# A four-layer decoder trunk: the two head-pair phases of its delta-rule layer become one timetable of 16 jobs

## The chip, the cores and the metric

The kernel runs on one core of one Trainium2 chip. The metric is the device time of one execution in microseconds, the median of the runs. Each core has a TensorE for matmuls (PE in the profile, its weight loads PEld), a VectorE (DVE), a ScalarE (ACT), a GpSimd (POOL) and a SyncE (SP) that issues the transfers.

## The reference

Four layers run one after the other over 1024 tokens of 1024 channels: a gated short convolution, a diagonal state-space layer, a delta-rule layer, and a second convolution. After each mixer come a gated embedding and a LayerNorm. Only the third layer's mixer is touched. Cut to what matters:

```python
def _rwkv_step(state, inp):
    r_t, w_t, k_t, v_t, kk_t, a_t = inp
    sa = jnp.einsum("bhvk,bhk->bhv", state, -kk_t)
    state = (state * w_t[:, :, None, :] + sa[..., None] * (kk_t * a_t)[:, :, None, :]
             + v_t[..., None] * k_t[:, :, None, :])
    return state, jnp.einsum("bhvk,bhk->bhv", state, r_t)

def rwkv7_mixer(x, ...):                    # 16 heads of 64
    xs = x[None] + dx[None] * mu[:, None, None, :]          # six mixes of x with its shift
    r, k, v, z = jnp.einsum("nbld,nde->nble", xs[:4], w_rkvz)
    w_log = -softplus(-(w0 + tanh(xs[4] @ w1) @ w2)) - 0.5   # the decay, low rank
    a = sigmoid(a0 + (xs[5] @ a1) @ a2)
    kk = normalised(k * k_k);  k = k * (1 + (a - 1) * k_a)
    _, out = lax.scan(_rwkv_step, s0, (r, decay, k, v, kk, a))   # over 1024 tokens
    out = group_norm(out) * lnx_g + lnx_b + sum(r * k * r_k) * v
    return (out * silu(z)) @ w_out
```

## The kernel before

All data is float32. A projection of 512 tokens onto 128 channels is 24 matmuls of 128x512: the weights and the inputs are each split into a rounded high part and a rest, and three of the four products are summed over eight blocks of 128 input channels. `wsplit_hi` (a ScalarE cast of 128x1024) and `wsplit_lo` (a VectorE subtraction) split a block of weights, and `build` mixes, splits and stores eight blocks of an input (`xs3`, `xs2`, `xs1`, `xs0` for z, v, k, r).

The recurrence is computed in chunks of 64 tokens. The 1024 tokens fall into two halves of 512, the 16 heads into eight pairs that fill 128 partitions, so there are 16 jobs of one pair and one half, of eight chunks each. A job goes through four stages in four successive slots:

- as `c` it gets its key projection (`K`, psum `kps`) and the decays, and begins its receptance projection (`Rd`);
- as `b` it gets scaled keys `kb`, queries `ra`, the chunk scores `s1`, their masks and the bonus;
- as `a` the triangular matrices of its chunks are inverted: `solve` and `unfold` on VectorE, then `join1` to `join4` and `queries`, each some tiny matmuls whose result ScalarE copies to SBUF for the next;
- as `s` it runs the chunks one after the other: `read` is a matmul with the state, whose result ScalarE copies (`uv`), and `update` a second matmul, from which two VectorE instructions (L2173) make the new state.

In the slot behind that its outputs are normalised (`g`). A slot has 16 steps: an even one begins with `read`, an odd one with `update`. Within a slot the table of steps in `phase` sets the order on every engine, and `pin` holds the scheduler to it; outside `phase` a scheduler places what is ready. `phase(h, ...)` runs eight jobs of one half in 11 slots, n = -3 to 7, since four jobs are under way at once. It is called twice. In its last three slots, where no new projections start, it is given others to do (`fill`): in the first call the z projections of half 1, in the second the output projections of half 0.

The layer's order is: `lora(0)` (the two low-rank products), z and v of half 0, with `decay` for each channel block; `phase(0)`; `lora(1)`, v and decay of half 1; `phase(1)`; then output projection, gate and LayerNorm. z, v, decays and the bonus go through DRAM. PSUM has eight banks: two for projections (`pmm`), three for small products (`paux`), and in `pseq` two for a job's outputs (`p1`) and one for `update`.

Of the kernel before, what the change touches and what calls it, by code (L numbers as in the profile page):

```python
# [1349 lines left out]
def rwkv_layer(S, X, bg, l, last, nxt):  # L1350
# [136 lines left out]
    def k_decays(m, h, R):  # L1487
# [7 lines left out]
        SC.activation(R.kp, R.ga, AF.Identity, scale=vec("k_a")[:, m:m + 1], bias=C.oka[:, m:m + 1])
        G.tensor_tensor(R.ga, R.ga, R.cs, ALU.mult)

    def k_evac(m, h, R):
# [3 lines left out]
        V.scalar_tensor_tensor(c3(R.aq), c3(ps), C.nkk[:, m:m + 1], R.pt[:, :, 0:CH], ALU.mult, ALU.mult)
        SC.activation(R.kk, ps, AF.Copy, scale=vec("k_k")[:, m:m + 1])
# [51 lines left out]

    def r_low(R):
        G.tensor_tensor(R.kl, R.kp, f32(R.kh), ALU.subtract)
# [707 lines left out]
```

## Time and profile before

| | us |
|---|---|
| median of 3 runs (lowest, highest) | 2899.98 (2897.66, 2902.37) |
| the profiled execution | 2900.2 |
| its span, first to last instruction | 2898.5 |
| DVE / ACT / POOL busy in the span | 1796.8 / 1122.3 / 670.0 |
| delta-rule mixer, first projection to first gate matmul | 1145.6 to 2147.7 |
| phase 0, first to last `read` | 1352.7 to 1656.1 |
| phase 1, first to last `read` | 1833.9 to 2124.7 |

The layer is read in stretches, from one `read` of a slot's step 0 to the next: a view that gives the busy time of each engine in each stretch shows where it is slow. TensorE's busy time counts overlapping matmuls and their modelled ends, so it says little by itself. The granted clock of TensorE (PEclk, 1.00 is full) stands in the same rows.

### The profile page before, as it was taken

What the parts mean: (1) busy time and instruction counts of PE and PEld (TensorE: products, weight loads), DVE (VectorE), ACT (ScalarE), POOL (GpSimd) and SP (SyncE); (2) the same over time, 40 slices, a digit from 0 to 9 for tenths busy, and PEclk for the clock granted to TensorE, in tenths of its full rate; (3) what the DMA queues carried; (4) which work ended last, traced back from release to release, by engine and by line L of the source; (5) the groups of instructions that cost most, each with busy time, mean ns of one, the idle gap of its engine ahead of it and who ended that gap; (6) DMA issues with size and microseconds to landing.
All of it is one profiled execution on the core that took longest, in us unless ns stands there. A gap on an engine that the chain in (4) does not pass through costs nothing. (4 is left out here: it accounts for less than half of the span.)

```text
span 2898.5 us, 47059 instructions
## 1 busy us (share of the span) xinstructions
PE 2698.8 (93%) x18331; PEld 2162.0 (75%) x18331; DVE 1796.8 (62%) x3288; ACT 1122.3 (39%) x2154; POOL 670.0 (23%) x828
## 2 busy tenths in 40 slices
PE   8999999999999999978887986988889999999998
PEld 6887887778878887666775764777667778888887
DVE  6777865477657348866676486666657573333654
ACT  3333322242154124655555474555534231111322
POOL 1243413222107043004344101344232210000000
PEclk9999999999999999988887998999999999999999
DMA  5333322267873334542222353222234332112311
GB/s 165 100 97 92 97 71 66 88 179 208 224 239 106 102 91 131 164 160 84 73 86 80 119 156 119 76 80 90 94 111 137 109 88 58 51 44 66 117 64 39
DMA packets 449775, 313.09 MB, mean 108 GB/s; under 512 B 48360, under 2 KB 393744, under 8 KB 449552
## 3 DMA queue, kind: packets, MB, share of 16 engines
q1 hardware_dynamic: 449552, 310.08, 35.5%
q8 instruction: 144, 2.36, 0.3%
q14 instruction: 79, 0.65, 0.1%
HBM read 240.28 MB, written 69.21 MB: 107 GB/s over the span
## 5 line engine op out<-in xcount | busy, mean ns | idle before, releaser
L300 DVE TENSOR_TENSOR wl<-wraw,wh 128x1024 fp32r<-128x1024 f32 x283 | 367.1, 1298 | 338.9 <-ACT wh L292 332.8
L292 ACT CAST wh<-wraw 128x1024 fp32r<-128x1024 f32 x283 | 296.4, 1048 | 650.7 <-PE gp L335 189.7
L2173 DVE SCALAR_TENSOR_TENSOR state<-state,pc,p 64x64 f32<-64x64 f32 x256 | 70.9, 277 | 81.0 <-PE p L2170 76.6
L2164 PE MATMUL p<-state,ra 128*128 128x128 f32 x256 | 62.5, 329 | 52.7 <-DVE state L2173 52.7
L672 POOL TENSOR_TENSOR ln_s<-ln_s,rp 128x512 f32<-128x512 f32 x42 | 60.0, 1428 | 210.4 <-DVE rp L668 210.4
L2164 PEld LDWEIGHTS p<-state,ra 128*128 128x128 f32 x256 | 44.4, 205 | 79.5 <-DVE state L2173 72.9
L2165 ACT COPY uv<-p 64x128 f32<-64x128 f32 x128 | 33.1, 258 | 141.5 <-PE p L2164 140.4
L334 PE MATMUL gp<-r_0h,wh 128*128 128x512 f32 x192 | 76.8, 400 | 0.9 <-ACT yt L2226 0.9
L336 PE MATMUL gp<-r_0h,wl 128*128 128x512 f32 x192 | 77.3, 403 | 0.0
L334 PE MATMUL zp<-x_0h,wh 128*128 128x512 f32 x192 | 76.8, 400 | 0.0
L335 PE MATMUL gp<-r_0l,wh 128*128 128x512 f32 x192 | 76.7, 400 | 0.0
L334 PE MATMUL gp<-r_1h,wh 128*128 128x512 f32 x192 | 76.3, 397 | 0.0
L336 PE MATMUL gp<-r_1h,wl 128*128 128x512 f32 x192 | 76.0, 396 | 0.0
L336 PE MATMUL zp<-x_0h,wl 128*128 128x512 f32 x192 | 75.9, 395 | 0.0
L334 PE MATMUL zp<-x_1h,wh 128*128 128x512 f32 x192 | 75.9, 395 | 0.0
L336 PE MATMUL zp<-x_1h,wl 128*128 128x512 f32 x192 | 75.7, 394 | 0.0
L335 PE MATMUL zp<-x_0l,wh 128*128 128x512 f32 x192 | 75.7, 394 | 0.0
L335 PE MATMUL zp<-x_1l,wh 128*128 128x512 f32 x192 | 75.6, 394 | 0.0
L335 PE MATMUL gp<-r_1l,wh 128*128 128x512 f32 x192 | 75.4, 393 | 0.0
L687 POOL TENSOR_TENSOR rp<-r_0h,r_0l 128x512 f32<-128x512 f32 x24 | 37.4, 1590 | 163.3 <-PE op L335 162.9
L2170 PEld LDWEIGHTS p<-uv,kbt 128*128 128x128 f32 x256 | 49.2, 209 | 25.5 <-ACT uv L2165 17.5
L2170 PE MATMUL p<-uv,kbt 128*128 128x128 f32 x256 | 56.4, 305 | 11.5 <-ACT uv L2165 11.5
(760 smaller groups left out, 8392.4 us busy)
## 6 DMA issues: line engine op xcount, KB each, us to landing
wraw<-in_conv_w_in_dram SPq DMA_DIRECT2D x80, 512.0 KB
wraw<-in_rwkv_w_rkvz_dram SPq DMA_DIRECT2D x64, 512.0 KB
wraw<-in_ple_gate_dram SPq DMA_DIRECT2D x56, 512.0 KB
wraw<-in_conv_w_out_dram SPq DMA_DIRECT2D x24, 512.0 KB
wraw<-in_ssm_w_in_dram SPq DMA_DIRECT2D x21, 512.0 KB
xt<-xd SPq DMA_DIRECT2D x32, 256.0 KB
wraw<-in_rwkv_w_out_dram SPq DMA_DIRECT2D x16, 512.0 KB
wraw<-in_ple_proj_dram SPq DMA_DIRECT2D x14, 512.0 KB
```

The lines of the kernel that those rows point to most:

```text
L292: S.nc.scalar.copy(wh, raw)
L300: S.nc.vector.tensor_tensor(wl, raw, f32(wh[:]), ALU.subtract)
L334: nc.tensor.matmul(ps, lh, xh, start=(k == 0), stop=False)
L335: nc.tensor.matmul(ps, lh, xl, start=False, stop=False)
L336: nc.tensor.matmul(ps, ll, xh, start=False, stop=(k == kt - 1))
L672: nc.gpsimd.tensor_tensor(s, s, rs, ALU.add)
L687: (eng or nc.gpsimd).tensor_tensor(rs, f32(rh[:]), f32(rl[:]), ALU.add)
L2164: nc.tensor.matmul(p1, R.ra[:, c, :], R.st, start=False, stop=False, skip_group_check=True)
L2165: SC.copy(R.uv[w][rb, c2, :], p1[rb, :])
L2170: nc.tensor.matmul(p2[:, 0:P], R.kbt[c // 4][:, c % 4, :], R.uv[w][:, c2, :], start=True, stop=True)
L2173: V.scalar_tensor_tensor(R.st[cs, cs], R.st[cs, cs], R.pc[cs, c:c + 1], p2[cs, cs], ALU.mult, ALU.add)
```

## The change

Both halves go through one `phase` of 16 jobs in 19 slots, n = -3 to 15; the job of a half 1 pair takes its state from DRAM as before. z of both halves and v of both halves are computed ahead of it, and v's weights are loaded and split once for both halves. The fill of the last three slots is the output projection of half 0 alone, by a table `NE`; `NK` and `NR` spread the 24 matmuls of K and R over other steps. The inputs of half 1 (`xs1`, `xs0`) are built inside slots 5 and 6, those of r of half 0 in slot -3.

Inside a slot nearly everything moves to another step. A product and the copy of its result out of PSUM become two functions (`join1` and `join1_out`, and so on), and a weight block's cast (`high`, steps 4 and 9) and subtraction (`low`, steps 7 and 13) stand apart. `solve` 3 moves from step 15 to the next slot's step 1, `solve` 0 from step 14 to step 13, the joins from steps 5 to 8 to steps 8 to 13, `queries` from 10 to 14. `p1` shares a pool of five banks with the small products.

Some instructions change: the ScalarE copy `kk` goes, and VectorE multiplies `kps` itself; the second copy of `queries` goes from VectorE to ScalarE; every job takes the group norm's root from ScalarE's Ln and Exp with a refinement on GpSimd, where jobs with m of 5 and more had another routine; the rest `kl` of the bonus is computed twice, by two equal GpSimd instructions.

```diff
-            for h in range(2):
-                for i in (3, 2):
-                    blocks("rwkv_w_rkvz", (0, i))
+            for i in (3, 3, 2):
+                blocks("rwkv_w_rkvz", (0, i))
+            for h in range(2):
...
-    S.paux = pss.enter_context(S.tc.tile_pool(name="paux", bufs=3, space=PSUM))
+    S.paux = pss.enter_context(S.tc.tile_pool(name="paux", bufs=5, space=PSUM))
...
     def k_evac(m, h, R):
-        SC.activation(R.kk, ps, AF.Copy, scale=vec("k_k")[:, m:m + 1])
...
+    def k_keys(m, R):
...
+        kk = T_("kk")
+        V.scalar_tensor_tensor(kk, R.kps, vec("k_k")[:, m:m + 1], R.ga, ALU.mult, ALU.mult)
...
+        V.tensor_tensor(view(R.kb, 0, [[256, 4], [192, 2], [1, 64]]), c4(kk), c4(prn), ALU.mult)
...
     def r_bonus(m, h, R):
...
         G.tensor_tensor(R.kl, R.kp, f32(R.kh), ALU.subtract)
 
+        G.tensor_tensor(R.kl, R.kp, f32(R.kh), ALU.subtract)
...
-    def phase(h, builds, fill, late):
+    def phase(fill, work):
...
+        def high():
+            if len(S.wready) + len(S.whalf) <= 1 and len(S.worder) > len(S.wready) + len(S.whalf):
+                wsplit_hi(S)
+                wnext(S)
+
+        def low():
+            if S.whalf:
+                wsplit_lo(S)
...
+        NR = 4, 4, 6, 6, 0, 0, 0, 0, 0, 0, 0, 0, 0, 2, 0, 2
+        NK = 0, 0, 0, 0, 3, 6, 6, 1, 2, 1, 0, 3, 2, 0, 0, 0
...
-        for n in range(-3, NB):
+        for n in range(-3, NP):
...
     def queries(R):
...
-        SC.copy(r5[:, :, 0, acol[0]], ps[0][:, 0:256].rearrange("p (c t) -> p c t", c=4))
-        V.tensor_copy(r5[:, :, 1, acol[1]], ps[1][:, 0:256].rearrange("p (c t) -> p c t", c=4))
+    def queries_out(R):
+        r5 = R.ra.rearrange("p (c w) s -> p c w s", w=2)
+        for w in range(2):
+            SC.copy(r5[:, :, w, acol[w]], R.pq[w][:, 0:256].rearrange("p (c t) -> p c t", c=4))
...
     def values(R):
-        R.p1 = [S.pseq.tile([P, 4, P], F32, tag="p1", name="p1", bufs=2) for w in range(2)]
+        R.p1 = [aux("p1").rearrange("p (a b) -> p a b", a=4) for w in range(2)]
...
+    for m in range(NB):
+        use_z(m, 0, zv_mm(zw(m), 3, m, 0))
+        pull(bg, ZP[m])
+    L = [lora(0)]
+    while bg:
+        pull(bg)
+    x1_load()
+    for _ in build(S, X, 3, 1):
+        pass
+    nxt_b.append(build(S, X, 2, 0))
+    for m in range(NB):
+        use_z(m, 1, zv_mm(zw(m), 3, m, 1))
+        decay(m, 0, L[0])
+        pull(nxt_b)
...
+    L.append(lora(1))
+    for _ in build(S, X, 2, 1):
         pass
+    for m in range(NB - 2):
+        w = vw(m)
+        for h in range(2):
+            use_v(m, h, zv_mm(w, 2, m, h))
+        decay(m, 1, L[1])
...
+    spread(build(S, X, 0, 0), -3, (1,) * 8, 4)
+    work[(NB - 4, 14)] = [x1_load]
+    spread(build(S, X, 1, 1), NB - 3, (2, 2, 1, 1, 1, 1), 4)
+    spread(build(S, X, 0, 1), NB - 3, (1, 1, 1, 1, 1, 1, 2), 12)
+    spread(ys_build(0), 2 * NB - 4, (1, 0, 0) + (1,) * 8, 13)
+    phase(wos, work)
```

How the order moves at three places. First VectorE in the middle of a slot, around the state's instruction (L2173 before, L2228 now, two 64x64 halves in a row); `wl` is the weight subtraction, `sca` the masked scores, `ra` the queries, `kp` the bonus product. Before:

```order
L1550 SCALAR_TENSOR_TENSOR kp<-sp,vec_174,kp 128x512
L2173 SCALAR_TENSOR_TENSOR state<-state,pc,p_13550 64x64 x2
L1980 TENSOR_TENSOR sca<-s_13578,mask 128x4x64
L1980 TENSOR_TENSOR sca<-s_13577,mask 128x4x64
L300 TENSOR_TENSOR wl<-wraw,wh 128x1024
L2173 SCALAR_TENSOR_TENSOR state<-state,pc,p_13636 64x64 x2
L1980 TENSOR_TENSOR sca<-s_13641,mask 128x4x64
L1980 TENSOR_TENSOR sca<-s_13640,mask 128x4x64
L2138 COPY ra<-a_13667 128x4x64
L2173 SCALAR_TENSOR_TENSOR state<-state,pc,p_13693 64x64 x2
```

Now:

```order
L2228 SCALAR_TENSOR_TENSOR state<-state,pc,p_14378 64x64 x2
L1554 SCALAR_TENSOR_TENSOR kp<-sp,vec_174,kp 128x512
L2006 TENSOR_TENSOR sca<-s_14386,mask 128x4x64
L2006 TENSOR_TENSOR sca<-s_14385,mask 128x4x64
L300 TENSOR_TENSOR wl<-wraw,wh 128x1024
L2228 SCALAR_TENSOR_TENSOR state<-state,pc,p_14463 64x64 x2
L2006 TENSOR_TENSOR sca<-s_14468,mask 128x4x64
L2006 TENSOR_TENSOR sca<-s_14467,mask 128x4x64
L2228 SCALAR_TENSOR_TENSOR state<-state,pc,p_14567 64x64 x2
L2038 STREAM_TRANSPOSE mi<-dg 128x1024
```

The subtraction `wl` stands ahead of the state of chunk 4 in both; before, it was step 8's, now it is step 7's `low`, whose cast is from step 4 (below). The copy `ra<-a` is gone from this queue.

Second ScalarE, around that weight block's cast `wh` (L292 before, L293 now); `uv` is the copy that follows a `read`, `tt`, `t` and `zi` belong to the joins, `kph` to the bonus, `gsq` or `junk` to the group norm. Before, from step 6 to step 9:

```order
L1552 CAST kph<-kp 128x512
L2197 ACTIVATE gsq,gn_q<-o 128x64
L2117 COPY t_13535<-zp 32x256 x2
L1982 COPY scr<-s_13578 128x4x64
L1982 COPY scr<-s_13577 128x4x64
L1342 ACTIVATE rs_t<-gn_q 128x8
L1343 ACTIVATE gn_s<-rs_t 128x8
L2165 COPY uv<-p_13263 64x128
L2125 COPY tt<-tp 32x8x32 x2
L292 CAST wh<-wraw 128x1024
L1993 COPY dg<-sca 32x256 x2
```

Now, from step 4 to step 8:

```order
L2220 COPY uv<-p_14184 64x128
L2253 ACTIVATE junk,gn_q<-o 128x64
L293 CAST wh<-wraw 128x1024
L2121 COPY uv<-wps 64x512 x2
L2253 ACTIVATE junk,gn_q<-o 128x64
L2220 COPY uv<-p_14185 64x128
L2253 ACTIVATE junk,gn_q<-o 128x64
L1556 CAST kph<-kp 128x512
L2253 ACTIVATE junk,gn_q<-o 128x64
L2220 COPY uv<-p_14184 64x128
```

The cast stood in the step of its subtraction, behind the copies of `join3`, the scores and `join4`; now it stands three steps ahead of it, behind one instruction of the group norm.

Third TensorE, at the joins: `zi`, `ut`, `zp` are the products of `join1` to `join3`, `p` is `read` (from state) or `update` (from uv), `sp` a projection. Before:

```order
L2087 MATMUL zi<-t_12288,nz_9823 32x32 x32
L2089 MATMUL zi<-ident 32x256 x4
L370 MATMUL sp<-xs1h,wh 128x512
L370 MATMUL sp<-xs1l,wh 128x512
L370 MATMUL sp<-xs1h,wl 128x512
L2164 MATMUL p_12164<-state,ra 128x128
L2098 MATMUL ut<-zi,ub 32x32 x32
L2101 MATMUL ut<-ub,zi 32x32 x32
L370 MATMUL sp<-xs1h,wh 128x512
L370 MATMUL sp<-xs1l,wh 128x512
L2170 MATMUL p_12450<-uv,kbt 128x128
L2115 MATMUL zp<-t_12435,m_11949 32x32 x16
```

Now, where `join2` and `join3` stand:

```order
L2219 MATMUL p_13636<-state,ra 128x128
L2142 MATMUL ut<-zi,ub 32x32 x32
L2145 MATMUL ut<-ub,zi 32x32 x32
L2225 MATMUL p_14018<-uv,kbt 128x128
L1565 MATMUL pb<-kph,c_ones_r 128x512
L1566 MATMUL pb<-kpl,c_ones_r 128x512
L371 MATMUL sp<-xs1l,wh 128x512
L371 MATMUL sp<-xs1h,wl 128x512
L371 MATMUL sp<-xs1h,wh 128x512
L2280 MATMUL otp<-ident,o 128x128 x4
L2219 MATMUL p_13635<-state,ra 128x128
L2164 MATMUL zp<-t_14022,m_13286 32x32 x16
```

Between `join2` and `join3` there stood two projection matmuls and an `update`; now there stand three, the bonus sum `pb`, four transposes `otp`, an `update` and a `read`.

More of the change, by code (lines that the diff above doesn't have):

```diff
@@ L25 @@
 VECS = {}
+AHEAD = 2
 class Ctx:
@@ L304, in wnext @@
 def wnext(S, ahead=2):
-    while len(S.wraws) < ahead and len(S.wready) + len(S.wraws) < len(S.worder):
+    while len(S.wraws) < ahead and len(S.wready) + len(S.whalf) + len(S.wraws) < len(S.worder):
         wdma(S)
@@ L1074 @@
 IP, TP, TQ = 5,2,2
-AHEAD = 2
 NU = 5
@@ L1783, in phase @@
                     if b:
+                        I.solve(b, 1)
                         I.solve(b, 2)
-                        I.solve(b, 3)
-                if n in (-3, 5) and i >= 4:
-                    thunk()
+                    if g:
+                        I.gate(g)
                 pin()
-        g = Rs[NB - 1]
+        g = Rs[NP - 1]
         I.square(g, 0, 8)
-        I.norm(g, h)
+        I.norm(g)
+        I.refine(g)
         I.scale(g)
@@ L1794, in phase @@
         I.affine(g)
-        I.gate(g, h)
+        I.gate(g)
         pin()
@@ L1893, in rwkv_layer, with spread @@
                  **w_out_then(m)) for m in range(NB)]
-    phase(1, build(S, X, 0, 1), wos, ys_build(0))
+    work = {}
+    def spread(g, n, counts, first=0):
+        for j, c in enumerate(counts):
+            for _ in range(c):
+                work.setdefault((n + (first + j) // 16, (first + j) % 16), []).append(lambda: next(g, None))
+    spread(build(S, X, 0, 0), -3, (1,) * 8, 4)
[4 more added lines that the diff above has]
+    phase(wos, work)
     while wos:
@@ L2226, in affine, with gate @@
         SC.activation(q4(R.yt), q4(R.po)[:, :, ::-1, :], AF.Identity, scale=gn[:, m:m + 1], bias=bn[:, m:m + 1])
-    def gate(R, h):
+    def gate(R):
         G.tensor_tensor(R.yt, R.yt, R.bv, ALU.add)
         G.tensor_tensor(R.yt, R.yt, R.z, ALU.mult)
-        nc.sync.dma_start(dY[R.m][:, h * HT:(h + 1) * HT], R.yt)
-    I.scores, I.mask, I.low_mask, I.diag, I.fold, I.scale_keys, I.kbt = scores, mask_, low_mask, diag, fold, scale_keys, kbt
-    I.solve, I.unfold, I.corr, I.corr_out = solve, unfold, corr, corr_out
-    I.join1, I.join2, I.join3, I.join4, I.queries, I.values = join1, join2, join3, join4, queries, values
-    I.init, I.read, I.update, I.outputs = init, read, update, outputs
-    I.square, I.norm, I.scale, I.turn, I.affine, I.gate = square, norm, scale, turn, affine, gate
+        nc.sync.dma_start(dY[R.m][:, R.h * HT:(R.h + 1) * HT], R.yt)
+    for f in (scores, low_mask, diag, off_diag, fold, scale_keys, loads, kbt, kbt_out, solve, unit, unfold, corr, corr_out,
+              join1, join1_out, join2, join2_out, clear, join3, join3_out, join4, join4_out, queries, queries_out, init, values,
+              read, update, outputs, outputs_out, square, norm, refine, scale, turn, affine, gate):
+        setattr(I, f.__name__, f)
+    I.mask, I.mask_r = mask_a, mask_r
     return I
```

502 lines of the change are left out of this document (250 added, 252 removed).

## The prediction

> **What bounds it now.** The page's head gives the span; the profiled execution took 2900.2 us, 0.01% from the runs' median of 2899.98, so the sum is made against 2900.2. About 6 us (0.2%) is what a measurement here can tell from no change.
>
> The view of stretches comes first, since only the delta-rule mixer is touched: per stretch its length, the busy time of each engine, the granted clock, and the transfers. The first 21 rows are slots and prologues in the order of the program (the last two of the fence are the first prologue).
>
> ```profile
> span 2898.5 us, 47059 instructions
> ...
> 1270.00:1352.70 82.70, 61.35 (x621) 48.09 (x619) 48.45 (x98) 42.78 (x78) 24.78 (x33) 0.79 0.29 91
> 1352.70:1388.30 35.60, 31.49 (x539) 25.25 (x535) 24.14 (x69) 18.91 (x43) 12.11 (x17) 1.00 0.19 57
> 1388.30:1427.40 39.10, 35.68 (x540) 29.09 (x538) 23.49 (x53) 22.14 (x62) 16.75 (x25) 0.87 0.20 67
> 1427.40:1469.20 41.80, 36.15 (x543) 29.32 (x539) 26.58 (x65) 22.15 (x62) 16.73 (x25) 0.88 0.25 79
> 1469.20:1508.20 39.00, 34.29 (x541) 27.76 (x539) 26.71 (x65) 22.04 (x62) 16.71 (x25) 0.91 0.28 84
> 1508.20:1548.20 40.00, 34.19 (x541) 28.19 (x539) 26.81 (x65) 22.03 (x62) 16.71 (x25) 0.91 0.43 135
> 1548.20:1601.20 53.00, 36.05 (x510) 28.80 (x506) 38.22 (x90) 27.39 (x71) 16.62 (x23) 0.68 0.20 59
> 1601.20:1635.10 33.90, 31.59 (x516) 25.60 (x512) 15.18 (x45) 17.44 (x47) 5.26 (x9) 1.00 0.33 104
> 1635.10:1670.00 34.90, 31.39 (x179) 24.49 (x177) 16.29 (x48) 15.37 (x53) 5.12 (x6) 1.00 0.46 137
> 1670.00:1690.00 20.00, 11.98 (x34) 4.18 (x34) 17.00 (x24) 17.20 (x28) 2.87 (x2) 0.84 0.42 124
> 1690.00:1745.30 55.30, 55.30 (x243) 43.53 (x243) 44.32 (x67) 36.45 (x68) 0.00 (x0) 0.96 0.54 176
> 1745.30:1833.90 88.60, 61.05 (x630) 46.90 (x628) 53.34 (x107) 45.59 (x84) 24.67 (x32) 0.83 0.30 103
> 1833.90:1868.90 35.00, 31.51 (x538) 25.49 (x534) 24.20 (x67) 19.02 (x43) 10.97 (x16) 1.00 0.21 63
> 1868.90:1906.30 37.40, 32.96 (x543) 26.95 (x539) 23.82 (x53) 22.05 (x62) 16.56 (x24) 0.95 0.21 69
> 1906.30:1945.30 39.00, 32.90 (x540) 26.90 (x538) 26.66 (x65) 22.05 (x62) 16.60 (x24) 0.96 0.26 85
> 1945.30:1987.60 42.30, 37.18 (x542) 30.58 (x538) 26.66 (x65) 22.14 (x62) 16.59 (x24) 0.84 0.24 78
> 1987.60:2026.50 38.90, 33.19 (x543) 26.77 (x539) 26.82 (x65) 22.04 (x62) 16.57 (x24) 0.96 0.31 92
> 2026.50:2066.50 40.00, 30.89 (x509) 24.63 (x507) 30.75 (x78) 21.81 (x63) 16.59 (x21) 0.83 0.36 115
> 2066.50:2100.60 34.10, 32.03 (x514) 25.42 (x512) 18.44 (x52) 16.21 (x46) 4.44 (x6) 1.00 0.27 86
> 2100.60:2137.00 36.40, 31.90 (x174) 25.35 (x173) 18.71 (x43) 15.21 (x52) 8.48 (x8) 0.95 0.35 109
> 2137.00:2147.70 10.70, 1.61 (x8) 0.79 (x6) 9.50 (x12) 1.89 (x3) 7.99 (x7) 0.69 0.48 148
> 1145.60:1233.00 87.40, 80.32 (x323) 54.58 (x322) 76.78 (x125) 54.30 (x95) 14.50 (x23) 0.96 0.53 163
> 1233.00:1270.00 37.00, 37.00 (x175) 29.84 (x174) 29.78 (x40) 22.70 (x34) 0.00 (x0) 1.00 0.71 232
> sum 1002.10, PE 841.98 PEld 658.50 DVE 672.65 ACT 548.89 POOL 287.65; mean PE 36.61 PEld 28.63 DVE 29.25 ACT 23.86 POOL 12.51
> ```
>
> The mixer takes 1002.1 us. Its eight full slots (n = 1 to 4 of each phase) take 39.7 us on average, and no engine fills one: DVE 24 to 27, ACT 22, POOL 17; PE's 33 to 37 counts overlaps and slow clock. So a slot is bound by waits in turn, not by an engine. The two ramps, in which the first job climbs three stages, cost 82.7 and 88.6 us.
>
> The same view by chunk (two steps each), for the slot that starts at 1987.6:
>
> ```profile
> 1987.60:1992.60 5.00, 2.73 (x24) 2.20 (x20) 4.78 (x19) 2.67 (x7) 1.27 (x1) 1.00 0.73 204
> 1992.60:1995.70 3.10, 2.57 (x12) 1.87 (x12) 2.88 (x8) 2.03 (x8) 0.00 (x0) 1.00 0.01 3
> 1995.70:2000.80 5.10, 4.58 (x114) 3.55 (x115) 4.90 (x11) 1.36 (x7) 0.00 (x0) 1.00 0.37 104
> 2000.80:2005.30 4.50, 4.41 (x183) 3.77 (x181) 0.62 (x3) 3.83 (x13) 1.85 (x3) 1.00 0.20 66
> 2005.30:2010.80 5.50, 3.56 (x57) 2.90 (x56) 2.79 (x5) 3.54 (x10) 3.79 (x9) 1.00 0.01 3
> 2010.80:2016.40 5.60, 5.58 (x50) 4.45 (x51) 2.54 (x7) 2.86 (x7) 3.68 (x7) 0.70 0.42 117
> 2016.40:2018.80 2.40, 2.40 (x13) 1.76 (x11) 2.32 (x3) 1.93 (x4) 0.19 (x1) 1.00 0.66 192
> 2018.80:2026.50 7.70, 7.37 (x94) 6.26 (x93) 5.99 (x12) 3.81 (x8) 5.78 (x4) 1.00 0.21 78
> ```
>
> A chunk can pass in 2.40 us. Chunks 0 and 2 are VectorE's (4.78 of 5.00, 4.90 of 5.10), 3 is TensorE's joins and scores, and in 4 nobody works through. The timeline shows why, and what slows VectorE in the last chunk of another slot, the one from 1868.9 (the fence ends with two groups of the four slots from there: busy us, mean ns, idle before):
>
> ```profile
> 2008.70 1.56 DVE L300 TENSOR_TENSOR wl<-wraw,wh 128x1024 fp32r<-128x1024 f32 x1 [2.64 <-ACT wh L292]
> ...
> 2010.82 0.49 PE L2164 MATMUL p<-state,ra 128*128 128x128 f32 x2 [1.97 <-DVE state L2173]
> ...
> 1900.13 1.90 POOL L2005 TENSOR_TENSOR kb<-kb,pc 128x1024 f32<-128x1024 f32 x1
> ...
> 1901.62 1.98 DVE L2036 TENSOR_TENSOR tp<-mi 128x192 f32<-128x192 f32 x2
> 1903.53 1.71 DVE L2039 TENSOR_TENSOR mi<-mi,tp 128x192 f32<-128x192 f32 x2
> ...
> L1557 POOL TENSOR_TENSOR kpl<-kp,kph 128x512 fp32r<-128x512 f32 x4 | 5.1, 1266 | 0.6 <-ACT kph L1552 0.3
> L1503 ACT ACTIVATE kk<-sp,vec 128x512 f32<-128x512 f32 x4 | 2.8, 690 | 3.6 <-DVE aq L1502 3.6
> ```
>
> `wl` waits 2.64 us for its cast, the state's instruction stands behind it, and `read` waits 1.97 us for the state. In the chunk after, the clock is 0.70.
>
> **The steady slot, from 39.7 us.** Removed: (a) the cast now stands three steps ahead of `wl`; of 2.64 us I take 2.0. (b) With that gap gone the slow chunk runs at full clock; 5.6 us at 0.70 is 3.9 at 1.00, and I take 1.2 of the 1.7. (c) The joins are spread from steps 5 to 8 over 8 to 14, each copy with a dense product or a read behind it; chunks 2 and 3 (9.6 us) lose 1.5. (d) In the last chunk 10 of its 12 projection matmuls go elsewhere (10 x 0.228 = 2.3 us, the 0.228 being 55.30 us over 243 in the row of v), `solve` 3 moves to step 1, and `solve` 0's four products (1.98 + 1.71) now stand ahead of GpSimd's big multiply; of some 4 us I take 2.5, since ScalarE now has nine copies in steps 13 to 15. Added: (e) chunks 0 and 1 get 20 of R's matmuls where eight stood, 12 x 0.228 = 2.7, of which VectorE's 4.78 and 2.88 there cover all but 1.0; (f) in step 14 `queries` takes two of the three banks that `p1` leaves free, as before, but `otp` now sits in the third until `affine`; `pss` behind it has to wait for a bank, and behind `pss` stand `update`, ScalarE and the state. I take 0.5, between 0 and the 1.97 that is the nearest wait shown. The ScalarE copy `kk` (0.69) goes and one of 128x256 comes; both lie beside a VectorE that is the later of the two. The second `kl` adds 1.27 us to a GpSimd that is busy 16.6 of 39: nothing. Balance: 39.7 - 2.0 - 1.2 - 1.5 - 2.5 + 1.0 + 0.5 = 34.0 us. The bounds: no gain, 39.7, and 31.0, if (a) to (d) give their full 2.6, 1.7, 2.0 and 4.0 and (e) and (f) 1.6.
>
> **The prologues.** z of half 0 had 87.4 us together with the low-rank products, decays and the previous layer's LayerNorm on a VectorE that was busy 76.78. Without the first two, 192 matmuls take 44 us and VectorE some 40: I take 50 (44 to 62). The low-rank stage now stands alone as half 1's did, 20.0 us (VectorE 17.00 of it), and the reading back of x adds 3: 23, bounds 14 and 30. z of half 1 with decays, 224 matmuls: 53, like the 55.3 of v with decays. The second low-rank stage: 20. v of both halves: 55.3 and another 192 x 0.228 = 44, less a first product under the low-rank stage: 95; the eight weight splits saved lie under it and are worth nothing. Sum 241, where 124.4 + 20 + 55.3 = 200 stood: z of half 1 is no longer under a phase's tail.
>
> **The phase.** One ramp, the mean of the two rows, 85 (75 to 95: same chains, other steps). Slot 0 at 35.3 x 34.0 / 39.7 = 30. Twelve full slots, n = 1 to 12: 408. The 16 inputs that slots 5 and 6 build: the 53.0 of slot 5, which built eight, against 39.7 is 13; VectorE's own part 38.22 - 26.7 = 11.5; half of the second eight lies in slot 6 under less: 20, bounds 12 and 27. The last three slots with the output projections, 40.0 + 34.1 + 36.4 = 110.5, less the gain of two slots: 99. The step to the gate stays, 10.7. Their queue of transfers moves too: key loads go from step 5 to step 2, v's from the transposes to step 0, all on SP, with a slot's 70 to 135 GB/s far from the 232 of a row above.
>
> Sum: 241 + 85 + 30 + 408 + 20 + 99 + 10.7 = 893.7, against 1002.1: -108, so 2792. Each us of the slot is worth about 15 (12 slots, and the outer ones in part).
>
> [...]
>
> **Rivals.** First, the slots stay at 39.7: the chain of `read`, copy, `update`, state may find another late partner at each place where one was removed, ScalarE above all. For it: no engine was full, so the waits may only wander. Against: (a) is a named wait whose cause moves away. The time: 15 x 5.7 = 85 more, 2878; still faster, since a ramp of 85 and the tail are saved and 41 given back.
>
> Second, the second `kl` counts: it runs in step 7 with `wl`, which reads two tiles of SBUF and took 1.56 at 2008.70 beside GpSimd's work; held up by 1.27 in each of 16 slots, ahead of the state, it costs 20: 2812.
>
> Third, slower: TensorE waits more often with fewer projections near its joins, and the granted clock falls in all slots as in slot 5, the row with 0.68 and 53.0 us. From a slot of 41.2 on (34.0 + 108 / 15) the gain is gone; TensorE's 33 us busy at 0.96 would be 41 at 0.77, so a mean of 0.77 decides. At 0.72 a slot is 44: 2942. Against: the slots of 33.9 and 34.1 us ran at 1.00, and full ones at 0.95 with the gap of (a) in them. [...]
>
> **Chances.** Forecast, slots of 31.5 to 37: 0.60, 2792, its own range 2755 to 2838. Slots unchanged: 0.16. The lock: 0.10. The slow clock: 0.14, of which 0.03 fall within 0.2%. Faster 0.86, the same 0.03, slower 0.11. The range takes in the unchanged slots above and slots of 31 below: 2745 to 2880, with 0.08 below and 0.12 above left out.
>
> **What would show it.** In the stretches: 12 slots of 33 to 35 us with the clock above 0.95; `wl` without a wait for `wh`; chunk 4 at 3.6 or less, the last at 5 to 6; a prologue of 235 to 250 us up to the first K product; one ramp of 85. The forecast is wrong if slots pass 37, if slot 5 exceeds 65, or if z of half 1 waits long for its inputs behind x's read-back.

## The result and the profile after

The changed kernel takes 2923.85 us against 2899.45 of the kernel before (medians): a ratio of 1.0081, 95% interval 1.0061 to 1.0101. It is slower by 0.8%, where 2792 us, 3.7% faster, had been forecast. The profiled execution took 2923.56 us. One of the four runs was in a slow state (3090.82 us at a mean clock of 0.823, where the other three had 0.951 or 0.952) and is left out of the ratio; the other three took 2922.15 to 2924.13.

The view of stretches, kernel after, in the same form as in the prediction (length; busy us of PE, PEld, DVE, ACT, POOL; granted clock; transfers). First the gap, z of half 0, the low-rank products, z of half 1, the low-rank products again, v, and the ramp:

```profile
1145.60:1152.70 7.10, 0.86 (x4) 0.38 (x2) 7.10 (x9) 4.12 (x6) 6.40 (x13) 0.80 0.69 163
1152.70:1206.60 53.90, 50.14 (x213) 39.67 (x213) 38.21 (x63) 17.78 (x27) 7.72 (x12) 0.96 0.55 174
1206.60:1222.60 16.00, 10.98 (x32) 3.94 (x32) 14.04 (x21) 14.13 (x24) 0.00 (x0) 0.86 0.63 187
1222.60:1284.90 62.30, 56.41 (x224) 42.99 (x224) 46.55 (x71) 42.50 (x78) 0.00 (x0) 0.91 0.53 171
1284.90:1300.00 15.10, 15.08 (x46) 5.12 (x48) 10.76 (x16) 9.16 (x15) 0.00 (x0) 0.84 0.01 5
1300.00:1406.00 106.00, 101.38 (x460) 80.47 (x456) 52.09 (x78) 39.76 (x74) 0.00 (x0) 0.98 0.43 149
1406.00:1495.30 89.30, 57.84 (x612) 44.29 (x612) 61.83 (x108) 50.99 (x94) 28.59 (x35) 0.83 0.28 88
```

Then slots of the one phase: n = 0, 1, 4, 5, 6, 9, 10, 13, and the last with the step to the gate:

```profile
1495.30:1528.60 33.30, 30.57 (x539) 25.58 (x535) 27.27 (x70) 18.58 (x43) 14.50 (x19) 1.00 0.19 59
1528.60:1570.70 42.10, 37.46 (x540) 31.78 (x538) 23.52 (x63) 22.24 (x63) 19.02 (x26) 0.83 0.22 70
1652.00:1694.10 42.10, 37.49 (x541) 31.93 (x539) 23.40 (x62) 22.19 (x62) 18.99 (x26) 0.82 0.40 129
1694.10:1760.70 66.60, 45.47 (x540) 35.82 (x538) 43.73 (x86) 37.07 (x86) 20.19 (x26) 0.71 0.17 54
1760.70:1809.00 48.30, 39.65 (x540) 32.59 (x538) 30.25 (x70) 26.95 (x70) 18.75 (x26) 0.82 0.18 60
1890.80:1933.00 42.20, 37.55 (x541) 31.98 (x539) 23.39 (x62) 22.21 (x62) 18.84 (x25) 0.82 0.25 78
1933.00:1972.60 39.60, 34.90 (x540) 29.77 (x538) 23.79 (x62) 22.09 (x62) 18.75 (x25) 0.89 0.27 85
2056.20:2093.70 37.50, 31.52 (x521) 25.45 (x519) 28.84 (x61) 23.07 (x65) 16.94 (x22) 0.89 0.30 93
2126.90:2171.00 44.10, 32.32 (x182) 25.46 (x180) 20.23 (x31) 18.54 (x58) 18.90 (x24) 0.92 0.43 131
```

VectorE's work in a full slot is 23.4 to 23.8 us (24 to 27 before), and yet the slots are longer: 41.3 us on average for the ten without builds, against 39.7, with a clock of 0.82 to 0.89. In n = 0, where no group norm runs yet, the clock is 1.00. The chunks of the slot from 1890.8 show where:

```profile
1890.80:1896.50 5.70, 5.70 (x31) 5.25 (x30) 1.45 (x4) 1.85 (x4) 1.15 (x1) 0.72 0.55 176
1896.50:1899.70 3.20, 3.20 (x17) 2.67 (x16) 2.54 (x9) 2.14 (x10) 0.13 (x1) 1.00 0.23 82
1899.70:1903.50 3.80, 3.80 (x46) 3.23 (x45) 2.78 (x11) 2.86 (x8) 0.00 (x0) 1.00 0.02 4
1903.50:1906.90 3.40, 3.40 (x29) 2.85 (x28) 3.23 (x9) 0.61 (x3) 0.00 (x0) 1.00 0.00 0
1906.90:1910.60 3.70, 3.70 (x97) 2.80 (x96) 2.66 (x7) 1.94 (x7) 2.82 (x2) 1.00 0.16 49
1910.60:1917.70 7.10, 5.13 (x142) 4.21 (x141) 3.10 (x5) 5.61 (x14) 6.46 (x14) 0.78 0.18 53
1917.70:1920.90 3.20, 3.19 (x74) 2.64 (x73) 1.78 (x4) 2.16 (x5) 0.85 (x3) 0.96 0.22 82
1920.90:1933.00 12.10, 9.44 (x116) 8.34 (x114) 5.86 (x19) 5.03 (x12) 7.42 (x8) 0.66 0.33 100
```

Chunks 1 to 4 run as forecast: 14.1 us together, with nothing idle on TensorE. Chunk 5 (7.10, where 5.6 had stood) and chunk 7 (12.10, where 7.7 had stood and 5 to 6 were forecast) take it all back. The timeline of these two, from the middle of the slot to its end:

```profile
1907.55 1.21 DVE L300 TENSOR_TENSOR wl<-wraw,wh 128x1024 fp32r<-128x1024 f32 x1
1907.70 2.20 POOL L1559 TENSOR_TENSOR kpl<-kp,kph 128x512 fp32r<-128x512 f32 x1 [11.07 <-ACT kph L1556]
1909.97 1.27 POOL L1561 TENSOR_TENSOR kpl<-kp,kph 128x512 fp32r<-128x512 f32 x1
1911.33 0.24 POOL L2256 TENSOR_SCALAR gn_q<-gn_q 128x8 f32<-128x8 f32 x1
1911.60 0.21 ACT L2258 ACTIVATE rs_t<-gn_q 128x8 f32<-128x8 f32 x1 [2.64 <-POOL gn_q L2256]
...
1912.79 1.04 ACT L293 CAST wh<-wraw 128x1024 fp32r<-128x1024 f32 x1
1913.86 0.26 ACT L2220 COPY uv<-p 64x128 f32<-64x128 f32 x1
1914.17 0.50 PE L2225 MATMUL p<-uv,kbt 128*128 128x128 f32 x2 [1.97 <-ACT uv L2220]
...
1923.88 0.62 ACT L1516 COPY ra<-aq 128x512 f32<-128x512 f32 x1 [1.27 <-DVE aq L1506]
1924.52 0.65 ACT L2193 COPY ra<-a 128x256 f32<-128x256 f32 x2
1924.94 1.87 PE L1512 MATMUL pss<-c_ones_r,sq 128*128 128x2 f32 x8 [2.49 <-ACT ra L2193]
1926.67 0.78 PE L2225 MATMUL p<-uv,kbt 128*128 128x128 f32 x2
```

`wl` has lost its wait, as intended. But in step 8 ScalarE stands 2.64 us at the group norm's Ln, since GpSimd has both `kl` to do before the norm's small addition; behind the Ln stand the second cast `wh`, `uv` and so TensorE's `update`, which comes 1.97 us late. In step 14 `pss` waits 2.49 us until ScalarE has emptied a bank of `queries` (L2193), with `update` behind it. After each of the two TensorE runs slow. The same view, cut at the edges of the clock:

```profile
1911.10:1914.50 3.40, 1.43 (x130) 1.28 (x118) 0.02 (x1) 2.78 (x8) 2.99 (x8) 1.00 0.25 73
1914.50:1917.93 3.43, 3.43 (x13) 2.78 (x11) 2.80 (x4) 2.83 (x8) 3.19 (x7) 0.50 0.00 0
1917.93:1921.34 3.41, 3.35 (x74) 2.60 (x73) 2.00 (x4) 2.58 (x7) 1.07 (x2) 1.00 0.20 77
1921.34:1924.75 3.41, 0.98 (x32) 0.77 (x32) 3.07 (x7) 2.07 (x5) 3.19 (x6) 1.00 0.51 146
1924.75:1928.17 3.42, 3.23 (x24) 3.00 (x26) 0.64 (x3) 1.39 (x4) 3.34 (x3) 0.50 0.05 13
1928.17:1931.58 3.41, 3.41 (x40) 3.08 (x38) 1.71 (x10) 1.16 (x2) 0.46 (x1) 0.50 0.31 95
1931.58:1935.00 3.42, 3.42 (x37) 3.30 (x36) 0.00 (x0) 0.78 (x2) 0.00 (x0) 0.50 0.84 265
```

In this view the clock changes only at the edges of stretches of 3.40 to 3.43 us. The stretch in which TensorE was busy for 1.43 us and the one with 0.98 are each followed by one at 0.50; after the second, two more stay slow, although TensorE works all through them, mostly on small products. So here a wait of 1.97 us was followed by 3.43 us at half clock, and one of 2.49 us by 10.25.

The sum by the prediction's terms, in us of the two profiled executions (forecast, then measured from the starts of the `read`s):

| term | forecast | measured | difference |
|---|---|---|---|
| prologue, 1145.6 to the first K product at 1406.0 | 241 | 260.4 | +19.4 |
| ramp | 85 | 89.3 | +4.3 |
| slot 0 | 30 | 33.3 | +3.3 |
| ten full slots, n = 1 to 4 and 7 to 12 | 340 | 412.7 | +72.7 |
| slots 5 and 6 with the builds | 88 | 114.9 | +26.9 |
| last three slots and the step to the gate | 109.7 | 114.8 | +5.1 |
| sum | 893.7 | 1025.4 | +131.7 |

The mixer took 1002.1 us before. Of the 26.9 in slots 5 and 6, 14.6 are two slots of 41.3 in place of 34.0, and 12.3 the builds, which cost 32.3 instead of 20. So 87 of the 132 us are the length of the slots.

### The profile page after: what moved, and what is told of

It reads as the page before. It is cut to its first block, busy times and chain, and to the rows that moved or that the text cites. A ratio compares the mean times of both kernels' runs of the same rounds, so it can differ in the third digit from the quotient of the medians.

```text
span 2921.7 us, 46913 instructions
## 1 busy us (share of the span) xinstructions
PE 2726.0 (93%) x18331; PEld 2201.4 (75%) x18331; DVE 1753.4 (60%) x3198; ACT 1114.3 (38%) x2156; POOL 712.7 (24%) x866
## 4 chain that ended last, share of the span: by engine, by line
PE 67%; issue 11%; DVE 11%; ACT 5%; POOL 2%; DMA 2%; SPq 0%; DVEq 0%; ACTq 0%; POOLq 0%
PE sp L371 4%; PE op L334 3%; PE op L335 3%; PE op L336 3%; PE gp L336 3%; PE gp L334 3%; PE gp L335 3%; PE zp L334 2%; PE zp L335 2%; PE zp L336 2%; PE hp L334 2%; PE hp L336 2%; PE hp L335 2%; PE cgp L334 2%; PE bp L334 2%
## 5 line engine op out<-in xcount | busy, mean ns | idle before, releaser
L293 ACT CAST wh<-wraw 128x1024 fp32r<-128x1024 f32 x275 | 288.1, 1048 | 695.7 <-PE gp L335 191.3
L300 DVE TENSOR_TENSOR wl<-wraw,wh 128x1024 fp32r<-128x1024 f32 x275 | 355.8, 1294 | 318.7 <-ACT wh L293 311.4
L2228 DVE SCALAR_TENSOR_TENSOR state<-state,pc,p 64x64 f32<-64x64 f32 x256 | 71.0, 278 | 207.5 <-PE p L2225 204.3
L1496 POOL COPY pc<-pt 128x8 f32<-128x8 f32 x16 | 15.1, 944 | 287.5 <-ACT pt L1494 272.0
L2225 PE MATMUL p<-uv,kbt 128*128 128x128 f32 x256 | 57.8, 311 | 26.3 <-ACT uv L2220 26.1
L1559 POOL TENSOR_TENSOR kpl<-kp,kph 128x512 fp32r<-128x512 f32 x16 | 33.2, 2078 | 197.0 <-ACT kph L1556 197.0
```

Of the source, the lines that this page charges most:

```text
L293: S.nc.scalar.copy(wh, raw)
L300: S.nc.vector.tensor_tensor(wl, raw, f32(wh[:]), ALU.subtract)
L2225: nc.tensor.matmul(p2[:, 0:P], R.kbt[c // 4][:, c % 4, :], R.uv[w][:, c2, :], start=True, stop=True)
L2228: V.scalar_tensor_tensor(R.st[cs, cs], R.st[cs, cs], R.pc[cs, c:c + 1], p2[cs, cs], ALU.mult, ALU.add)
```

## Experiments

All times are medians, beside runs of the kernel before on the same chip; ratios are to that kernel. The runs form three groups of four, in the order given here, each on another chip, on which the kernel before took 2898.38, 2899.20 and 2895.82 us: a few us between runs of different groups say nothing. "Theory W" says that the two waits make the slots long, with rivals beside it. The edits are to the changed kernel.

**One `kl`.** The second of the two subtractions goes:

```diff
         G.tensor_tensor(R.kl, R.kp, f32(R.kh), ALU.subtract)
-
-        G.tensor_tensor(R.kl, R.kp, f32(R.kh), ALU.subtract)
```

> Edit: the second of the two equal GpSimd subtractions `kl` is left out; the output is unchanged. Theory W (two waits set the slot; in step 10 ScalarE stands at the group norm's Ln until GpSimd has passed both `kl`, and the cast `wh`, `uv` and `update` stand behind it): the norm's small GpSimd instruction comes 1.3 us earlier, TensorE's wait of 1.97 us ahead of `update` falls to 0.6, chunk 5 of a full slot goes from 7.0 to about 5.4: 12 slots times 1.4 to 2.0, -17 to -24 us against the changed kernel (2923.6), so about 2903. Theory C (the slots are long because TensorE has too few projections in steps 8 to 15 and its clock is low by itself): the wait is no cause; -5 us at most, chunk 5 stays above 6.5. Theory L (VectorE is locked out by GpSimd's `kl`): `wl` gets shorter than its 1.21 us and the state behind it earlier, chunk 4 falls below 3.4.

Measured: 2882.72 us, ratio 0.9942 (0.9926 to 0.9958): 41 us less than with two, twice what was expected. The wait at the Ln halves (chain of waits of one slot):

```profile
ACT rs_t L2258 <- POOL gn_q L2256: 1.3, 1, 1.3
```

Chunk 5, 5.6 to 7.1 before, is 4.3 in nine of the ten full slots, and chunk 7 went from about 12 to between 10 and 11.8. `wl` stays at 1.21 to 1.23 us. So a GpSimd instruction of 1.27 us, on an engine busy 19 of 42, cost 1.3 in the queue and more in clock (0.91 in the two slots from 1830.3 on, where the full slots had 0.82 to 0.89); VectorE was not held up by it, and theory L falls.

**The norm early.** The last square and the norm's first half move to the head of step 7:

```diff
                 elif i == 7:
+                    if g:
+                        I.square(g, 7, 8)
+                        I.norm(g)
                     if b:
                         I.scores(b, 0)
                         r_bonus(b.m, b.h, b)
...
-                    if g:
-                        I.norm(g)
```

> Edit: the last square and the group norm's first half (GpSimd's small add, ScalarE's Ln and Exp) move from steps 7 and 8 to the head of step 7, ahead of the bonus, so ahead of both `kl` in GpSimd's queue and ahead of `kph` in ScalarE's; both `kl` stay. Theory W: ScalarE no longer waits 2.64 us at the Ln; `uv` of chunk 5 comes at about 1911 instead of 1913.9 in the slot from 1890.8, TensorE's wait of 1.97 us goes, and chunk 5 falls from 7.0 to 3.5 to 4.5: 12 times 2.5 to 3.5, -30 to -42 us, about 2887. Theory C: the clock in chunk 5 stays under 0.8, chunk 5 above 5.5, -15 us at most. Theory L: nothing, since both `kl` are still there.

Measured: 2884.63 us, 0.9952 (0.9938 to 0.9967): 39 us less, with both `kl` in place. Chunk 5 is 4.5 in nine of the ten full slots. So with the norm ahead of them the two `kl` no longer lengthen chunk 5, which is about as short as with one: what the second cost there came through the norm behind it. Chunk 7 still takes 10.6 to 12.3.

**`pss` late.** The products of the key norm move behind `update` and the outputs:

```diff
                 elif i == 14:
...
-                        k_norm(c)
                         k_query(c)
...
                 elif i == 15:
                     if s:
                         I.outputs(s)
...
+                        k_norm(c)
                         k_rnorm(c)
```

> Edit: the products `pss` of the key norm move from step 14 to step 15, behind `update` and the outputs on TensorE. Theory W (`pss` waits 2.49 us for the bank that `queries_out` gives back, with `update` behind it, and TensorE then runs the whole of step 15 at half clock): `update` of chunk 7 follows `queries` at once, chunk 7 falls from 12.0 to 6 to 8: 13 times 4 to 6, -52 to -78 us, about 2858. Theory B (a wait for a bank only moves: `values` then waits for the same banks): the 2.5 us come back ahead of `values`, chunk 7 stays above 10, -25 us at most. Theory C: chunk 7 has few projections and a clock of 0.66 with or without the wait: only the 2.5 us go, chunk 7 at 9.5, -32 us.

Measured: 2849.84 us, 0.9835 (0.9819 to 0.9852): 74 us less. A full slot, and its chunks 5 and 7:

```profile
1842.50:1876.60 34.10, 30.95 (x540) 26.07 (x538) 24.97 (x63) 22.09 (x62) 18.84 (x26) 1.00 0.32 99
1860.70:1866.30 5.60, 3.66 (x141) 3.00 (x141) 1.65 (x5) 4.37 (x12) 5.07 (x12) 1.00 0.26 77
1869.80:1876.60 6.80, 5.93 (x116) 5.12 (x114) 5.60 (x14) 4.93 (x12) 6.50 (x8) 1.00 0.48 145
```

That is the forecast slot, 34.1 us at full clock, in nine of the ten full slots (n = 1 takes 37.2). Theory B falls (`values` did not inherit the wait), and so does theory C, since the projections stand where they stood. `pss` still waits for the same copy, but only 0.6 us and with no `update` behind it.

**Both moves.**

> Edit: the two moves together (norm early, `pss` late). Theory W: the gains add: -82 to -120 us, about 2820, full slots of 33 to 35 us at a clock above 0.93. Theory C: full slots stay at 38 or more with a clock under 0.88, 2880 or more. If the two waits hide each other, less than the sum of the single runs.

Measured: 2844.28 us, 0.9814 (0.9800 to 0.9829): 5.6 below `pss` late alone, not the 39 that a plain sum would give. Chunk 5 is 4.5, but the slots are 33.2 to 35.0 and the clock no longer 1.00:

```profile
1865.20:1868.30 3.10, 3.09 (x74) 2.51 (x72) 1.95 (x4) 2.43 (x6) 2.93 (x6) 1.00 0.22 85
1868.30:1876.00 7.70, 6.60 (x115) 5.77 (x113) 6.50 (x15) 4.77 (x11) 7.32 (x8) 0.86 0.46 128
```

Most of the shorter slots now meet a slow stretch of 3.4 us in chunk 7 or 0 (0.50 from 1873.9 to 1877.3 in this one), with no wait of TensorE over 0.8 us in the slot. So the gains do not add, and theory W was too simple there: what a wait costs depends on the clock behind it.

**One `kl` and `pss` late.**

> Edit: `pss` late and one `kl` instead of two. `pss` late alone took 2849.84, one `kl` alone 2882.72. Theory G (a wait costs much only where it empties the stretch that decides the clock; with `pss` late the clock is 1.00 in all full slots): only the wait itself is saved, 1.3 us in 13 slots at the most, 2833 to 2850; and as the slots then change their length against the clock's steps of 3.4 us, some may turn slow again, as with both moves (2844.28). If the gains simply add (-41 and -74): 2809.

Measured: 2844.23 us, 0.9808 (0.9791 to 0.9826), full slots of 32.9 to 34.8: the second `kl` costs 41 us in one surrounding and 5.6 in the other, which is no more than a measurement here can tell from nothing.

**The wait kept and filled.** Four of R's matmuls stand in step 14 ahead of `pss`, which still waits for its bank:

```diff
-        NR = 4, 4, 6, 6, 0, 0, 0, 0, 0, 0, 0, 0, 0, 2, 0, 2
+        NR = 2, 2, 6, 6, 0, 0, 0, 0, 0, 0, 0, 0, 0, 2, 4, 2
...
+                    dense(i)
                     if c:
                         k_norm(c)
                         k_query(c)
-                    dense(i)
```

> Edit: four of R's projection matmuls move from steps 0 and 1 to step 14, ahead of `pss` on TensorE (NR 2, 2, 6, 6 and then 2, 4, 2); `pss` still waits for its bank, `update` still stands behind it. It parts the wait from the clock. In the changed kernel TensorE stands still from 1922.46 to 1924.94 and then runs at 0.50 until 1934.99. Theory G (most of chunk 7's loss is the slow clock that follows a half-empty stretch; `pss` comes no earlier, but what follows runs at full clock): chunk 7 from 12.1 to 8 to 9, 13 slots times 3 to 4, -39 to -52 us against 2923.6, so about 2878; clock in chunk 7 from 0.66 to above 0.9. Theory W alone (the wait is the loss): the wait stays, -10 us at most.

Measured: 2880.62 us, 0.9942 (0.9920 to 0.9963), 43 us less. Chunk 7 of two neighbouring slots:

```profile
1927.10:1935.30 8.20, 6.89 (x120) 5.71 (x118) 6.17 (x18) 4.79 (x11) 7.14 (x8) 1.00 0.33 99
1962.80:1976.10 13.30, 10.61 (x120) 9.05 (x118) 6.94 (x19) 5.00 (x12) 7.45 (x7) 0.69 0.27 84
```

The same instructions take 8.2 us where the clock holds and 13.3 where it does not. The wait of TensorE ahead of `pss` is not the same in the two, 1.3 us in the first and 2.6 in the second, so of the 5.1 us between them 1.3 are wait and most of the rest clock. Six of the ten full slots have 8.2 to 8.5, the other four 11.5 to 13.3. The loss in chunk 7 was thus mostly clock, and the fill holds the clock there in six of ten. But only half of the gain lies there: over the ten full slots chunk 7 loses 17.0 us and chunk 0, which has four matmuls fewer, 17.4. How much of that is the matmuls and how much the clock, no run separates.

**`affine` early.** It empties the bank of `otp` two steps sooner, and `pss` stays where it was:

```diff
                 elif i == 12:
...
+                    if g:
+                        I.affine(g)
                 elif i == 13:
...
-                    if g:
-                        I.affine(g)
```

> Edit: `affine`, the ScalarE instruction that empties `otp`, moves from the end of step 14 to the end of step 12; `pss` stays in step 14, ahead of `update`. Theory B5 (the bank of `otp` is what `pss` lacks; with five banks, two for `p1`, two for `queries`, the fifth is `otp`'s until `affine`): `pss` gets its bank before `queries_out`, `update` of chunk 7 comes at 1922.8 instead of 1926.7, chunk 7 falls from 12 to 6.5 to 8, like the run with `pss` late: -50 to -70 us, about 2862. 0.79 us of ScalarE now lie ahead of `pt` and `sq`, which may cost 0 to 0.8 us a slot. If `pss` waits for ScalarE for another reason than a bank, nothing: 2915 to 2930.

Measured: 2861.40 us, 0.9861 (0.9838 to 0.9883), 62 us less. No wait ahead of `pss` is left in the full slots, and chunk 7 is 6.6 to 8.2. So what `pss` lacked was the fifth bank, as term (f) had it; theory B5 holds.

**Builds one to a step** (with `pss` late):

```diff
-    work[(NB - 4, 14)] = [x1_load]
-    spread(build(S, X, 1, 1), NB - 3, (2, 2, 1, 1, 1, 1), 4)
-    spread(build(S, X, 0, 1), NB - 3, (1, 1, 1, 1, 1, 1, 2), 12)
+    work[(4, 12)] = [x1_load]
+    spread(build(S, X, 1, 1), NB - 3, (1,) * 8, 0)
+    spread(build(S, X, 0, 1), NB - 3, (1,) * 8, 8)
```

> Edit: `pss` late, and the 16 input builds of half 1 go one to a step through slot 5 (k in steps 0 to 7, r in 8 to 15) instead of two a step from step 4 and one from step 12; x is loaded two steps earlier. Compared with `pss` late alone (2849.84), where slots 5 and 6 took 62.9 + 43.2 = 106.1 us against 68.2 for two steady ones. Theory S (the builds cost much because K waits for them in the step they are made, 6.1 us of TensorE's waits on `xs1h`, and two chains ACT-DVE-ACT-DVE of 2.7 us stand in one step): the two slots fall to 86 to 94, -12 to -20 us, about 2834; bounds are VectorE's own 76 us of work there and no gain. Rival: each build costs ScalarE and VectorE the same wherever it stands, since each holds both in turn: within 5 us of 2850.

Measured: 2846.52 us, 0.9819 (0.9800 to 0.9838). Slots 5 and 6 take 105.8 us where they took 106.1: theory S falls, the rival was right. The chain of waits of slot 5 says what a build costs (ScalarE's cast waiting for VectorE's mix):

```profile
ACT xs0h L192 <- DVE mix L1322: 12.9, 8, 4.8
ACT xs1h L192 <- DVE mix L1322: 10.2, 8, 2.0
```

**Builds cut in two.** The cast and subtraction of a build move one step behind its mix:

```diff
+    for k in range(NB + late):
+        if late and k:
+            hl = (slot(S, t0, f"xs{s}h", F32R), slot(S, t1, f"xs{s}l", F32R))
+            split_into(S, hl, t)
+            xs.append(hl)
+        if k < NB:
+            t = mix(S, X, s, h, k)
...
```

> Edit: `pss` late; the 16 builds spread one to a step as in the run before (2846.52, slots 5 and 6 together 105.8 us), but each build is cut in two: ScalarE's and VectorE's mix stand in one step, the cast and the subtraction in the next, so that neither engine stands still for the other inside a build. Theory P (a build costs 37.6 / 16 = 2.35 us because ScalarE's cast waits up to 2 us for VectorE's mix, with `uv` and all else behind it): each costs 1.0 to 1.5 us, as much as the 1.34 us of ScalarE's two instructions; slots 5 and 6 together 84 to 92, -14 to -22 us, about 2829. Rival V (VectorE's own work, 75.5 us in the two slots, and the slow clock of 0.7 set it): 98 or more, within 8 us of 2847.

Measured: 2833.72 us, 0.9778 (0.9760 to 0.9796); the two slots:

```profile
1669.80:1725.70 55.90, 40.19 (x542) 31.51 (x538) 51.34 (x94) 40.21 (x93) 22.12 (x27) 0.81 0.21 65
1725.70:1762.60 36.90, 33.87 (x541) 28.63 (x539) 24.93 (x64) 22.73 (x63) 18.30 (x26) 0.91 0.27 81
```

92.8 us instead of 105.8, just above the expected 84 to 92: theory P holds for these 13 us, and a build costs (92.8 - 68.2) / 16 = 1.5 us instead of 2.35. In slot 5 VectorE is now busy 51.34 of 55.90 us, so the work of VectorE that rival V named is what is left there.

**The cast back beside its subtraction** (with `pss` late): term (a) undone alone.

```diff
                 elif i == 4:
...
-                    high()
...
                         I.mask(b, 0)
+                    high()
                     low()
```

> Edit: `pss` late, and the cast `wh` of steps 4 goes back beside its subtraction in step 7 (the cast of step 9 stays): term (a) of the prediction undone by itself. By the prediction `wl` then waits for its cast again, the state behind it and `read` behind that: +2.0 to +2.6 us in each of 14 slots, +28 to +36 us on 2849.84, about 2881; with a slow stretch of the clock behind it more. Rival: the state of chunk 3 comes early enough now, or GpSimd's `kl` hides it: +0 to +8.

Measured: 2839.64 us, 0.9798 (0.9782 to 0.9814), no slower than `pss` late with 2849.84 (0.9819 to 0.9852). `wl` does wait again, and the slot does not care:

```profile
1853.56 1.23 DVE L300 TENSOR_TENSOR wl<-wraw,wh 128x1024 fp32r<-128x1024 f32 x1 [1.21 <-ACT wh L293]
1837.00:1871.20 34.20, 31.48 (x543) 26.18 (x539) 25.13 (x63) 22.19 (x62) 18.94 (x26) 1.00 0.31 96
```

Chunk 4 grows by 0.5 us to 4.2, and chunk 5, which waits for the Ln in any case, shrinks by 0.5 to 5.1. The two profiled executions differ by 5.2 us, and that lies outside the steady slots: slots 0 and 1 are 4.5 us shorter and begin 2.0 earlier. What makes them so was not tried.

**All waits.** One `kl`, norm early, `pss` late, and the four matmuls in step 14.

> Edit: one `kl`, norm early, `pss` late, and four of R's matmuls in step 14 in place of steps 0 and 1. Theory G (with the waits gone, what is left are slow stretches of 3.4 us where TensorE has only small products, steps 14 and 15; four projection matmuls there keep the clock): chunk 0 3.2, chunk 5 4.3, chunk 7 6.7 to 7.5, full slots 32 to 33 us at a clock above 0.97: 12 times 1.7 less than with both moves (2844), about 2823, between 2812 and 2845. If the slow stretches only wander to other steps: 2835 to 2850.

Measured: 2808.18 us, 0.9687 (0.9668 to 0.9706). That is below the expected range of 2812 to 2845. Full slots take 30.9 us, where 32 to 33 were expected:

```profile
1790.50:1821.40 30.90, 30.60 (x541) 26.00 (x539) 25.07 (x63) 22.28 (x62) 17.70 (x25) 1.00 0.36 113
```

Chunk 5 is 3.5, chunk 0 3.2, chunk 7 6.8; TensorE is idle 0.3 us in the whole slot. How much of the gain is the norm's, the one `kl`'s or the four matmuls', no run separates.

**All waits and the cut builds.**

> Edit: the kernel of `e10_all_waits` with the builds of `e9_split_builds`. If the two gains add: about 2806, between 2790 and 2830, 3% below the kernel before the change.

Measured: 2791.05 us, 0.9631 (0.9610 to 0.9651): faster than both kernels, by 3.7% and 4.5%. Slots 5 and 6 take 52.8 and 32.4 us. The time is inside the expected range and 15 us below the plain sum of the gains. That it meets the forecast of 2792 is chance: shorter slots pay for a longer prologue.

## Why the prediction was wrong

The step that failed is term (f), `pss` in step 14. The place, the mechanism and those who stand behind it were named, and the run with `affine` early shows that the bank is the cause. Its size was taken as 0.5 us between 0 and 1.97. Over the ten full slots it measured 412.7 - 344.3 = 68.4 us by the run with `pss` late, 6.8 a slot, and 412.7 - 360.4 = 52.3 by `affine` early, 5.2 a slot: a wait of 2.49 us itself, above the upper bound, and then the half clock, 0.50 for 10.25 us in the slot shown. Of the 6.8, 5.1 lie in chunk 7 and the rest in chunks 0 and 5, with the other chunks little changed. The bound came from the nearest wait in the trace, although the length of this one could have been reckoned in the order: `queries_out` stands on ScalarE behind a copy that waits for VectorE's `aq`, behind `wl` and `solve` 0. And the clock behind a wait, which term (b) priced for the old wait, was not priced for the new one.

The second step is "the second `kl` adds 1.27 us to a GpSimd that is busy 16.6 of 39: nothing". The busy share was no cover: the instruction stands ahead of the norm's addition, and ScalarE's queue waits for that. Alone it costs 41 us; with the wait of `pss` removed 5.6, which can hardly be told from nothing.

The other terms of the slot, against the chunks of the slot from 1987.6 before:

- (a), 2.0: the wait of `wl` is gone and chunk 4 fell from 5.5 to 3.7, but by the run with the cast back the cast's place is worth 0.5 in chunk 4, and nothing in a slot whose chunk 5 waits for the Ln in any case. The other 1.3 come from what else left that place; no run separates them.
- (b), 1.2: did not come. The clock of chunk 5 went to 0.78; with the waits gone it is 1.00.
- (c), 1.5: chunks 2 and 3 went from 9.6 to 7.2, 2.4 less.
- (d), 2.5: without the wait of `pss` chunk 7 is 6.8 against 7.7, 0.9 less.
- (e), 1.0: chunks 0 and 1 went from 8.1 to 8.9, at a clock of 0.72 in chunk 0; with `pss` late they are 7.3.

Chunk 6, for which the prediction had no term, went from 2.4 to 3.2, and to 3.5 with `pss` late. With `pss` late the slot is 34.1 in nine of ten, beside the forecast of 34.0; but (b), (c), (d) and (e) are each off and chunk 6 was left out, and they cancel. That this sum met the slot is luck.

The builds: 20 with bounds 12 and 27, measured 32.3 in slots 5 and 6. VectorE's own added work there is 43.73 + 30.25 - 2 x 23.6 = 26.8 us, already more than the 20. On top of it ScalarE and VectorE wait for each other inside each build: the pair of runs with builds shows 13.0 us for that with `pss` late. What remains with the builds cut in two, 24.6 us, is about VectorE's own added work there (51.34 + 24.93 - 2 x 25.0 = 26.3).

The prologue: 260.4 for 241, read from the trace and not tested by a run. z of half 0 starts 7.1 us late, while VectorE is full with the layer before (the first row), and takes 61 with it instead of 50. z of half 1 takes 62.3 instead of 53, at a clock of 0.91, after a wait for the first of its inputs, which lies in the row before it (timeline):

```profile
1222.63 1.22 PE L334 MATMUL sp<-xs3h,wh 128*128 128x512 f32 x2 [5.05 <-ACT xs3h L192]
```

This wait is not for x's read-back: ScalarE begins the first mix at 1220.12, as soon as it is done with the casts of the low-rank stage (`lhl`, 1.26 us from 1218.84). v takes 106 instead of 95; the second half's 32 transposes had not been counted. The two low-rank stages were shorter than taken, 16.0 and 15.1 for 23 and 20.

The rivals. The third, slower by the clock, came nearest: from slots of 41.2 on the gain is gone, and they are 41.3. Its cause, fewer projections near the joins, was not what decided, since the same projections run at 1.00 with `pss` late; whether they count once the waits are gone, the runs do not separate (34.6 with one `kl` and `pss` late, 30.9 with the norm early and four matmuls moved besides). The second, called the lock among the chances, foresaw that the second `kl` costs, by the wrong way: in the full slots `wl` is not lengthened beside it (1.21 to 1.22 us). GpSimd's first `kl` is, to 2.20 us. Of the signs listed for a wrong forecast two showed as written, slots above 37 and slot 5 above 65 (66.6). The third showed in part: z of half 1 waits 5.05 us for its inputs, but behind the low-rank products and not behind x's read-back.

## What to carry to other kernels

When a step is moved in a hand-written order, ask of each instruction that takes a PSUM bank which instruction frees one, and reckon on that engine's queue when it can run; a bound taken from another wait is no bound. An engine that is half idle can still hold up another by the one small instruction at the end of its queue (here GpSimd, busy 19 of 42 us: 1.27 us more ahead of it cost 41). Where TensorE's clock falls after a wait as it did here (0.50 for 10.25 us after one of 2.49), price a wait with the slow stretch behind it, test removed waits together (one `kl` and `pss` late: 41 and 74 us less alone, 80 together), and move some dense work into the steps that have none (four matmuls moved to step 14: 43 us less, and chunk 7 at 8.2 to 8.5 in six of the ten full slots).
